# Other hidden pairs of a gated feed-forward projection take the seven-product form, and the sums of stored weights are issued at other moments

## The chip, the cores and the metric

The kernel runs on one core of a Trainium2 chip. Its engines work side by side: TensorE (PE, with its weight loads listed as PEld), VectorE (DVE), ScalarE (ACT), GpSimd (POOL) and SyncE (SP), which issues most of the transfers. The metric is the device time of one execution in microseconds (us); less is better. The runs before the change took 695.11 us in the median of three (695.10, 695.11 and 695.49).

## The reference

One layer of a streaming encoder on 512 positions of width 1024, all in float32. The part that the change touches is the channel mixer at the end:

```python
def causal_dwconv(x, w):            # 3 taps along the sequence
    K = w.shape[0]; S = x.shape[1]
    xp = jnp.pad(x, ((0, 0), (K - 1, 0), (0, 0)))
    y = xp[:, K - 1:K - 1 + S, :] * w[K - 1]
    for k in range(K - 1):
        y = y + xp[:, k:k + S, :] * w[k]
    return y
...
        x = x + (g_conv * y_conv + g_attn * y_attn) @ w_o[l]
        h = rms_norm(x, norm_ffn_g[l])
        up = causal_dwconv(h @ w_up[l], conv_ffn_w[l])      # 2 * 2816 columns
        a, b = jnp.split(up, 2, axis=-1)
        x = x + (jax.nn.silu(a) * b) @ w_down[l]
    return rms_norm(x, norm_f_g)
```

In front of it stand a gated short convolution and an attention branch, which the change leaves as they are.

## The kernel before, in words

**Precision.** Every float32 operand is split into a rounded high part and a rest, and a product is taken as three matmuls: high by high, rest of the weight by high, high weight by the rest of the activation. For each chunk of weights, `split()` has ACT write the high part (`wh`, line 274) and DVE the rest (`wl`, line 278) from the loaded `raw` tile. `wh` and `wl` have two buffers each, so a chunk can be split while PE works on the one before it, once PE has done with the one before that. `raw` has four buffers for P and up chunks together, and `rf` four for F chunks. Loads stand in SP's queue up to seven chunks ahead (`LOOK`), each waiting for its buffer.

**The up stage.** The 2816 hidden columns make 22 pairs `j` of two blocks, one block of `a` and one of `b`, in two phases: pairs 0 to 11, then 12 to 21. After each phase come the down products of that phase (`STEPS`, 12 and 8 steps). A normal pair is two chunks `up2j` and `up2j+1`; each block is 48 matmuls of 128 columns by 256. DVE takes the block out of its bank (`mul`, tile `fz`), multiplying by the norm; `taps` makes the convolution: one ACT instruction (line 565) and two on DVE (lines 566 and 569) into `fu`. `glu` then has ACT take the Silu of `a` (line 1212), and POOL multiplies by `b`: into `ge` for an even pair, into `go` for an odd one (lines 1217 and 1224). At an odd pair, DVE makes four sums of 128x256 out of `ge` and `go` (lines 1234 to 1239), and ACT and DVE split the results into `gh` and `gl` (lines 1243 and 1244): these are the operands of the seven-product down steps.

**Seven-product pairs.** For the pairs in `SUP`, `seven` computes both blocks for both halves of the sequence with seven products in place of eight. The pair is four chunks: P, F, P, F. A P chunk has 18 matmuls and an F chunk 24; in each, PE first does all that use `wh` (12 and 16) and then those that use `wl`. An F chunk is a set of four sums of weights, made by transfers inside DRAM and loaded like a weight. `merge` then puts the two blocks together from four banks on DVE (tiles `uz`, `ua`, `uu`, `ub`, lines 1173 to 1195). In names of rows, P12, F12, P13, F13 are the chunks of the first such pair, P14 to F15 those of the second, P16 to F17 those of the third.

**Order of the work around it.** Much of DVE's work is not issued at once but put on the list `later` with a time in us and a tag: `("e",)` for evacuations of a pair (out of the banks, taps, `glu`), `("q", q)` for the sums and splits of the gated values, `("x", q)` for those of the up stage's own operands. `run_later` takes from that list behind each split, up to a budget; `flush` and `flush_only` empty it for a tag or a bank.

**Sums of stored weights.** `make_forms` makes the F sums of a group of two steps by six transfers: `put` (SP) and `add` (POOL, adding into DRAM) in turn. `slot()` is called at each of the eight blocks of the output projection and twice at each pair, and issues what has come due: transfer `k` of group `g` is due at slot `step * k + shift * g`. `GROUPS` holds `(size, step, shift)`; key 0 is the down weights of phase 0: six groups, tiles `f18` to `f28`.

The kernel's functions that the change touches:

Of the kernel before, what the change touches and what calls it, by code (L numbers as in the profile page):

```python
# [58 lines left out]
PLAIN = [(m, k) for m in (6, 7) for k in range(*PHASES[1])]  # L59
PCUTS = (0, 8, 12, 20)  # L60

SUP = (1, 2, 5)
XF = 26
UPD = tuple(((j, q), (j, q + 1)) for j in SUP for q in (0, 2))
DOUBLES = GATES + UPD + STEPS[0] + STEPS[1]
N0 = len(GATES) + len(UPD)
GROUPS = {"gate": (2, 4, 1), "up": (2, 4, 1), 0: (2, 4, 1), 1: (2, 3, 1)}


@with_exitstack  # L70
def block_kernel(ctx, tc, xT, vecs, wv, win, wmix, wo, wup, wst, wdp, outT):
# [55 lines left out]
    n = 0  # L127
# [28 lines left out]
    later = []  # L156
# [31 lines left out]
    made, todo_bg = {}, []  # L188

    def make_forms(n0, n1, key):  # L190

        size, step, shift = GROUPS[key]
        make_forms.slot = 0
        cuts = [n0]
        for n in range(n0 + 1, n1 + 1):
            if n == n1 or n - cuts[-1] == size or len(DOUBLES[n]) != len(DOUBLES[cuts[-1]]):
                cuts.append(n)
        for g, (a, b) in enumerate(zip(cuts, cuts[1:])):
            m = len(DOUBLES[a]) * P
            f = dr.tile([P, b - a, 4 * m], F32, tag=f"f{a}", name=f"f{a}")  # L200
            w = wst[a:b].rearrange("n p c -> p n c")
            x0, x1, x2 = w[:, :, 3 * m : 5 * m], w[:, :, 5 * m : 7 * m], w[:, :, 7 * m : 8 * m]
            for n in range(a, b):
                made[n] = f[:, n - a, :]

            def put(dst, src):
                return lambda: keep(nc.sync.dma_start(dst, src))

            def add(dst, src):
                return lambda: keep(nc.gpsimd.dma_start(dst, src, accum_op=ALU.add))  # L210

            f0, f1, f2 = f[:, :, : 2 * m], f[:, :, 2 * m : 3 * m], f[:, :, 3 * m :]
            ops = (put(f0, x0), add(f0, x1), put(f1, f[:, :, :m]), add(f1, x1[:, :, m:]), put(f2, f1), add(f2, x2))
            todo_bg.extend((make_forms.slot + step * k + shift * g, op) for k, op in enumerate(ops))
        todo_bg.sort(key=lambda w: w[0])

    def slot():
# [18 lines left out]
    def flush(banks=None):  # L236

        def wanted(w):
            return set(w[2]) & set(banks) if banks is not None else True

        while any(map(wanted, later)):
            n = next(n for n, w in enumerate(later) if banks is None or wanted(w) or w[0] < len(parts))
            with after_split():
                later.pop(n)[3]()

    def flush_only(tags):

        while n := [n for n, w in enumerate(later) if set(w[2]) & set(tags)]:
            with after_split():
                later.pop(n[0])[3]()  # L250
# [137 lines left out]
    at = ExitStack()  # L388
# [62 lines left out]
    for kb in range(KB):  # L451
        x = xs[kb]
# [234 lines left out]
    n = 4 * H  # L687
    bf, me, mo = vec[:n, BF : BF + 1], vec[:n, ME : ME + 1], vec[:n, MO : MO + 1]
    z, e, o = (ap.tile([n, S], F32, tag="pp", name=nm, bufs=NPP) for nm in ("fz", "fe", "fo"))
# [56 lines left out]
    acc, bank_s, bank_t = ring(2, 0, 1), ring(3, 4), ring(5, 6)  # L746
# [25 lines left out]
    k = len(parts) + 2  # L772
    for q in (0, 2):
        f, g = x_sums(slice(q, q + 2))
# [8 lines left out]
    for idx in late:  # L783
        kind, i = divmod(idx, 4)
# [32 lines left out]
    def split_next():  # L817
        if len(parts) == chunk.n and stream[chunk.n][0] not in ("dp1", "dp2"):
            split()
# [288 lines left out]
    def turns(*ids):  # L1108
        st = list(ids)

        def f(name):
            f.last = st.pop(0)
            flush((f.last,))
            return bank(f.last, name)

        return f

    acc = turns(0, 1, *(2, 3, 4, 5) * 2, 6, 7, 0, 1, 2, 3, 4, 5)
    USETS = {1: (2, 3, 4, 5), 2: (6, 7, 0, 1), 5: (6, 7, 0, 1)}
    ssq3 = xp.tile([P, S], F32, tag="ssq", name="ssq3")  # L1120

    def place(ph, q):
# [2 lines left out]
    def up(j, ph, rb2, pu=None):  # L1125
        uu = []

        def tap(i, z):
            u = fp.tile([P, S], F32, tag="fu", name=f"fu{j}{i}", bufs=3)
            taps(u, z, CF + 3 * (2 * j + i))  # L1130
            uu.append(u)

        if j in SUP:
            c = len(GATES) + 2 * SUP.index(j)
            slot()
            seven(
                UPD[c - len(GATES) :][:2], c, {j: USETS[j]}, up_form, of="x",
                done=lambda i, banks, ids: merge(ph, j, banks, ids, rb2, tap, uu),
            )
            slot()  # L1140
            return
        evacs = []
        for i in range(2):
            slot()
            p = pu[i] if pu else block(f"up{2 * j + i}", x1h, x1l, True)
            if i and j + 1 == PHASES[ph][1]:
                split_next()
            z = [None]

            def mul(i=i, p=p, z=z):  # L1150
                z[0] = fp.tile([P, S], F32, tag="fz", name=f"fz{j}{i}", bufs=4)
                nc.vector.tensor_mul(z[0], p, rb2)

            evac = [(0.7, mul), (1.4, lambda i=i, z=z: tap(i, z[0]))]
            if i:
                evac.append((0, lambda: glu(ph, j, uu)))
            if any(("e",) in w[2] for w in later):
                later.extend((0, us, (("e",), acc.last) if x == 0 else (("e",),), f) for x, (us, f) in enumerate(evac))
            else:
                for _, f in evac:  # L1160
                    f()
# [46 lines left out]
    def glu(ph, j, uu):  # L1208
        a, b = uu
        q, k = j // 2, len(parts) - 1  # L1210
        g0 = place(ph, q)
        nc.scalar.activation(a, a, AF.Silu)
        if j == NP - 1:
            nc.scalar.activation(tbl, a[: 4 * H, :1], AF.Sqrt, scale=0.0, bias=eps[: 4 * H])
        if j % 2 == 0:
            ge = glu.even = fp.tile([P, 2, 2 * P], F32, tag="ge", name=f"ge{q}", bufs=2)
            keep(nc.gpsimd.tensor_mul(ge, a.rearrange(halves_of, h=2), b.rearrange(halves_of, h=2)))  # L1217
            return
        flush_only([("q", x) for x in range(q)])
        ge = glu.even  # L1220
        go = fp.tile([P, 6, 2 * P], F32, tag="gr", name=f"go{q}")

        def mul(eng):
            return eng.tensor_mul(go[:, 0:2, :], a.rearrange(halves_of, h=2), b.rearrange(halves_of, h=2))

        if j + 1 < PHASES[ph][1]:
            keep(mul(nc.gpsimd))
        else:
            later.append((k + 3, 0.7, (("q", q),), lambda: mul(nc.vector)))
        b11, b12 = ge[:, 0, :], ge[:, 1, :]  # L1230
        b21, b22, t1, t2, t3, t4 = (go[:, i, :] for i in range(6))

        def t13():
            nc.vector.tensor_sub(t1, b11, b12)
            nc.vector.tensor_sub(t3, b22, b12)

        def t24():
            nc.vector.scalar_tensor_tensor(t2, t1, -1.0, b22, op0=ALU.mult, op1=ALU.subtract)
            nc.vector.scalar_tensor_tensor(t4, t2, -1.0, b21, op0=ALU.mult, op1=ALU.subtract)

        def hl(src, gs):
            def f():
                nc.scalar.activation(gh[:, gs, :], src, AF.Copy)
                nc.vector.tensor_sub(gl[:, gs, :], src, gh.bitcast(F32)[:, gs, :])

            return f


        d = (2, 3, 4) if j + 1 < PHASES[ph][1] else (4, 5, 6)
        w = [(d[0], 0.85, t13), (d[0], 0.85, t24), (d[1], 0.7, hl(ge[:, : 1 + ph, :], slice(g0, g0 + 1 + NF * ph, NF)))]  # L1250
        w += [(d[x > 0 and 2 or 1], 0.7, hl(go[:, x : x + 2, :], slice(g0 + 1 + x, g0 + 3 + x))) for x in (0, 4, 2)]
        for n, us, f in w:
            later.append((k + n, us, (("q", q),), f))

    def combine(ph, i, banks, ids):

# [47 lines left out]
    for ph, (j0, j1) in enumerate(PHASES):  # L1304
        if ph:
            flush()
            acc = turns(*X * 5)
        if ph:
            make_forms(N0 + len(STEPS[0]), len(DOUBLES), ph)
        for j in range(j0, j1):  # L1310
            pu = None
            if j == 0:
                nrm = {}

                def mid():
                    nrm["c"] = rstd_col([ssq2], NT, 6, "n2")

                def late():
                    nrm["b"] = rstd_sb(rstd_bc(nrm["c"], NT, 7, "n2"), "n2")

                pu = lead(["up0", "up1"], x1h, x1l, mid, late)
            up(j, ph, nrm["b"], pu)
        assert not todo_bg
        flush((("e",),))
        seven(
            STEPS[ph], N0 + ph * len(STEPS[0]), ({0: X, 1: Y, 3: X, 2: Y}, {0: X, 1: Y, 2: Y})[ph],
            lambda q, g: (gh[:, place(ph, q) + g, :], gl[:, place(ph, q) + g, :]),
            goes_on=HELD if ph == 1 else None, stays=HELD if ph == 0 else None,
            done=lambda i, banks, ids: combine(ph, i, banks, ids),
        )  # L1330
# [188 lines left out]
```

## Time and profile before

| | before |
|---|---|
| median of three runs | 695.11 us |
| the profiled execution | 696.87 us, its span 695.0 us |
| PE busy in the span | 685.8 us (99%) |
| DVE busy | 534.6 us (77%) |
| ACT busy | 360.7 us (52%) |
| POOL busy | 181.8 us (26%) |
| granted TensorE clock | 0.996 in the mean |

The busy time of PE counts matmuls that overlap, so it says when PE had work, not how well it used it. The rows of the waits and of the timeline give the places where it had none. In rows of the profile `x48` is a count, the first two numbers of a timeline row are start and length in us, and `[1.24 <-ACT wh_P L274]` says that the engine had been idle for 1.24 us and who ended that.

### The profile page before, as it was taken

What the parts mean: (1) busy time and instruction counts of PE and PEld (TensorE: products, weight loads), DVE (VectorE), ACT (ScalarE), POOL (GpSimd) and SP (SyncE); (2) the same over time, 40 slices, a digit from 0 to 9 for tenths busy, and PEclk for the clock granted to TensorE, in tenths of its full rate; (3) what the DMA queues carried; (4) which work ended last, traced back from release to release, by engine and by line L of the source; (5) the groups of instructions that cost most, each with busy time, mean ns of one, the idle gap of its engine ahead of it and who ended that gap; (6) DMA issues with size and microseconds to landing.
All of it is one profiled execution on the core that took longest, in us unless ns stands there. A gap on an engine that the chain in (4) does not pass through costs nothing.

```text
span 695.0 us, 14638 instructions
## 1 busy us (share of the span) xinstructions
PE 685.8 (99%) x5960; PEld 684.1 (98%) x5960; DVE 534.6 (77%) x833; ACT 360.7 (52%) x568; POOL 181.8 (26%) x195
## 2 busy tenths in 40 slices
PE   9999999999999999999999999999999999999996
PEld 9999999999999999999999999999999999999996
DVE  6677887877578778869778799888774677777794
ACT  5574765554554444546555455545443344445572
POOL 6124947542020201213513134210000313221000
PEclk9999999999999999999999999999999999999998
DMA  8528999553568586785899876455647686766513
GB/s 310 219 63 292 216 242 211 130 121 92 190 137 227 164 272 201 236 302 118 128 302 279 211 178 133 116 177 179 200 127 231 141 194 157 188 173 174 156 31 122
DMA packets 60019, 127.57 MB, mean 184 GB/s; under 512 B 5376, under 2 KB 27920, under 8 KB 59696
## 3 DMA queue, kind: packets, MB, share of 16 engines
q1 hardware_dynamic: 41880, 101.51, 44.6%
q0 software_dynamic: 16832, 23.93, 21.7%
q10 hardware_dynamic: 1240, 1.19, 0.5%
q8 instruction: 47, 0.77, 0.4%
q14 instruction: 20, 0.16, 0.1%
HBM read 124.45 MB, written 41.42 MB: 239 GB/s over the span
## 4 chain that ended last, share of the span: by engine, by line
PE 93%; DVE 3%; DMA 2%; ACT 0%; issue 0%; DVEq 0%; ACTq 0%
PE dn L326 23%; PE p_up L308 21%; PE p_in L308 14%; PE p_up L326 6%; PE p_wo L308 6%; PE yc L308 3%; PE ya L308 3%; DMA raw_P<-in_wst_dram 2%; PE pa L476 2%; PE pb L478 2%; PE p_q L308 2%; PE p_k L308 2%; PE o L657 2%; PE tp L640 1%; PE pdB L308 1%; PE pdA L308 1%
## 5 line engine op out<-in xcount | busy, mean ns | idle before, releaser
L308 PE MATMUL p_up<-x1h,wl_up 128*128 128x256 f32 x464 | 90.4, 276 | 0.0
L308 PE MATMUL p_up<-x1h,wh_up 128*128 128x256 f32 x464 | 90.3, 276 | 0.0
L308 PE MATMUL p_up<-x1l,wh_up 128*128 128x256 f32 x464 | 90.3, 276 | 0.0
L210 POOL DMA_DIRECT2D f<-in_wst_dram x60 | 70.9, 1349 | 1.5 <-DMA f<-f 1.2
L308 PEld LDWEIGHTS p_up<-x1h,wl_up 128*128 128x128 f32 x464 | 69.9, 188 | 0.0
L308 PEld LDWEIGHTS p_up<-x1l,wh_up 128*128 128x128 f32 x464 | 69.8, 188 | 0.0
L308 PEld LDWEIGHTS p_up<-x1h,wh_up 128*128 128x128 f32 x464 | 69.8, 188 | 0.0
L278 DVE TENSOR_TENSOR wl_F<-raw_F,wh_F 128x1024 fp32r<-128x1024 f32 (+1 forms) x38 | 51.1, 1343 | 18.9 <-ACT wh_F L274 18.9
L274 ACT ACTIVATE wh_up<-raw_up 128x1024 fp32r<-128x1024 f32 x38 | 40.2, 1057 | 47.5 <-PE p_up L308 41.8
L274 ACT ACTIVATE wh_F<-raw_F 128x1024 fp32r<-128x1024 f32 (+1 forms) x38 | 40.0, 1053 | 36.1 <-PE dn L326 26.5
L308 PE MATMUL p_in<-xgh,wh_in 128*128 128x256 f32 x288 | 56.8, 279 | 0.0
L1217 POOL TENSOR_TENSOR ge<-fu,fu 128x512 f32<-128x512 f32 x11 | 19.8, 1798 | 140.8 <-DVE fu L569 108.7
L308 PE MATMUL p_in<-xgh,wl_in 128*128 128x256 f32 x288 | 56.6, 278 | 0.0
L308 PE MATMUL p_in<-xgl,wh_in 128*128 128x256 f32 x288 | 56.5, 278 | 0.0
L278 DVE TENSOR_TENSOR wl_up<-raw_up,wh_up 128x1024 fp32r<-128x1024 f32 x38 | 46.3, 1220 | 10.9 <-ACT wh_up L274 10.8
L274 ACT ACTIVATE wh_P<-raw_P 128x768 fp32r<-128x768 f32 (+1 forms) x38 | 31.7, 834 | 36.7 <-PE dn L326 22.8
L278 DVE TENSOR_TENSOR wl_P<-raw_P,wh_P 128x768 fp32r<-128x768 f32 (+1 forms) x38 | 36.9, 970 | 17.2 <-ACT wh_P L274 11.5
L308 PEld LDWEIGHTS p_in<-xgh,wh_in 128*128 128x128 f32 x288 | 44.7, 188 | 0.7
L326 PE MATMUL dn<-gl,wh_F 128*128 128x256 f32 x192 | 45.1, 276 | 0.0
L326 PE MATMUL dn<-gh,wh_F 128*128 128x256 f32 x192 | 45.1, 276 | 0.0
L308 PEld LDWEIGHTS p_in<-xgl,wh_in 128*128 128x128 f32 x288 | 43.7, 188 | 0.0
L308 PEld LDWEIGHTS p_in<-xgh,wl_in 128*128 128x128 f32 x288 | 43.6, 188 | 0.0
(343 smaller groups left out, 2150.5 us busy)
## 6 DMA issues: line engine op xcount, KB each, us to landing
raw_up<-in_wup_dram SPq DMA_DIRECT2D x38, 512.0 KB, 5.0
raw_F<-f SPq DMA_DIRECT2D x37, 512.0 KB, 4.5
raw_P<-in_wst_dram SPq DMA_DIRECT2D x37, 384.0 KB, 4.8
raw_in<-in_win_dram SPq DMA_DIRECT2D x24, 512.0 KB, 3.6
f<-in_wst_dram POOLq DMA_DIRECT2D x37, 256.0 KB, 6.3
f<-in_wst_dram SPq DMA_DIRECT2D x18, 512.0 KB, 6.6
f<-in_wst_dram POOLq DMA_DIRECT2D x18, 512.0 KB, 8.0
f<-f SPq DMA_DIRECT2D x36, 256.0 KB, 6.1
```

The lines of the kernel that those rows point to most:

```text
L210: return lambda: keep(nc.gpsimd.dma_start(dst, src, accum_op=ALU.add))
L274: ins = nc.scalar.activation(hi, raw, AF.Copy)
L278: ins = nc.vector.tensor_sub(lo, raw, hi.bitcast(F32))
L308: keep(nc.tensor.matmul(out[:, cs], w, x[:, cs], start=start and i == 0 and c == 0, stop=stop and i == 2 and c == len(cut) - 1,))
L326: keep(nc.tensor.matmul(out, wl if x == 1 else wh, xl if x == 2 else xh, start=opens and bk not in seen, stop=closes and bk not in left,))
L476: keep(nc.tensor.matmul(pa[t][:, :VW], xt, w[:, VB:], start=start, stop=stop))
L478: keep(nc.tensor.matmul(pb[t], xt, w[:, :VB], start=start and t % 2 == 0, stop=stop and t % 2 == 1))
L640: keep(nc.tensor.transpose(tp[:, ks], pt[:, ks], ident))
L657: keep(nc.tensor.matmul(o[:, 2 * P * e + c0 : 2 * P * (e + 1)], w, x[:, kb, c0:], start=e == 0 and kb == 0 and i == 0, stop=e == 1 and kb ...
L1217: keep(nc.gpsimd.tensor_mul(ge, a.rearrange(halves_of, h=2), b.rearrange(halves_of, h=2)))
```

## The change

Three things change together.

- **Which pairs.** `SUP` names pairs 1, 4 and 8 in place of 1, 2 and 5, with other banks for them (`USETS`) and another order of banks for the normal blocks (`acc`). The number of matmuls, of splits and of loads is the same.
- **Where sums go in the list.** `glu` inserts the sums and splits of the gated values in front of the first entry tagged `("e",)` in `later`, where it used to append them. At the last pair of a phase, if evacuations are pending, they are flushed and one more chunk is split ahead; and in front of the down steps only `("e",)` entries are flushed, where `flush` also ran other entries of `later` that had come due.
- **When the down weights' sums are made.** The six transfers of a group come due at slots 0, 3, 14, 18, 22 and 26 (plus the group's number) in place of 0, 4, 8, 12, 16 and 20.

```diff
-SUP = (1, 2, 5)
+SUP = (1, 4, 8)
...
-GROUPS = {"gate": (2, 4, 1), "up": (2, 4, 1), 0: (2, 4, 1), 1: (2, 3, 1)}
+GROUPS = {"gate": (2, 4, 1), "up": (2, 4, 1), 0: (2, (0, 3, 14, 18, 22, 26), 1), 1: (2, 3, 1)}
...
-            todo_bg.extend((make_forms.slot + step * k + shift * g, op) for k, op in enumerate(ops))
+            todo_bg.extend((make_forms.slot + (step * k if isinstance(step, int) else step[k]) + shift * g, op) for k, op in enumerate(ops))
...
-    acc = turns(0, 1, *(2, 3, 4, 5) * 2, 6, 7, 0, 1, 2, 3, 4, 5)
-    USETS = {1: (2, 3, 4, 5), 2: (6, 7, 0, 1), 5: (6, 7, 0, 1)}
+    acc = turns(0, 1, 6, 7, 0, 1, 6, 7, 0, 1, 2, 3, 0, 1, 2, 3, 4, 5)
+    USETS = {1: (2, 3, 4, 5), 4: (2, 3, 4, 5), 8: (4, 5, 6, 7)}
...
             if i and j + 1 == PHASES[ph][1]:
                 split_next()
+                if any(("e",) in w[2] for w in later):
+                    flush_only((("e",),))
+                    split()
...
-        for n, us, f in w:
-            later.append((k + n, us, (("q", q),), f))
+        at = next((x for x, i in enumerate(later) if ("e",) in i[2]), len(later))
+        later[at:at] = [(k + n, us, (("q", q),), f) for n, us, f in w]
...
-        flush((("e",),))
+        flush_only((("e",),))
```

Two places show how instructions move. The first is SP's queue behind the loads of the first seven-product pair (`raw_P12` to `raw_F13`); `f18` to `f28` on both sides of the arrow are the sums of the down weights. Before:

```order
L182 DMA raw_F13_4526<-f12_2618 128x1024
L182 DMA raw_P14_4538<-in_wst_dram 128x768
L182 DMA raw_F14_4540<-f14_2619 128x1024
L207 DMA f18_3993<-f18_3993 256x256
L207 DMA f20_3994<-f20_3994 256x256
L207 DMA f22_3995<-f22_3995 256x256
L182 DMA raw_P15_4682<-in_wst_dram 128x768
L182 DMA raw_F15_4684<-f14_2619 128x1024
L182 DMA raw_up6_4712<-in_wup_dram 128x1024
L182 DMA raw_up7_4764<-in_wup_dram 128x1024
L207 DMA f24_3996<-f24_3996 256x256
L207 DMA f26_3997<-f26_3997 256x256
```

The same place of SP's queue after the change:

```order
L182 DMA raw_F13_4527<-f12_2618 128x1024
L182 DMA raw_up4_4539<-in_wup_dram 128x1024
L182 DMA raw_up5_4677<-in_wup_dram 128x1024
L182 DMA raw_up6_4705<-in_wup_dram 128x1024
L182 DMA raw_up7_4757<-in_wup_dram 128x1024
L182 DMA raw_P14_4851<-in_wst_dram 128x768
L182 DMA raw_F14_4853<-f14_2619 128x1024
L207 DMA f18_3993<-f18_3993 256x256
L182 DMA raw_P15_4923<-in_wst_dram 128x768
L182 DMA raw_F15_4925<-f14_2619 128x1024
L207 DMA f20_3994<-f20_3994 256x256
L182 DMA raw_up10_5000<-in_wup_dram 128x1024
```

Four plain loads now stand between the two seven-product pairs, and the copies inside DRAM come behind them, one at a time.

The second place is DVE at a seven-product pair that does not stand right behind another one: the third pair in the order before (pair 5, chunks P16 to F17) and the second now (pair 4, chunks P14 to F15). `fz31` is the block `b` of pair 3, `fu31` its taps. Before:

```order
L1152 TENSOR_TENSOR fz30_5140<-p_up6_4938,rb_n2_4660 128x512
L278 TENSOR_TENSOR wl_P16_5195<-raw_P16_4988,wh_P16_5194 128x768
L1244 TENSOR_TENSOR gl_3989<-go0_4930,gh_3988 128x512 x2
L278 TENSOR_TENSOR wl_F16_5227<-raw_F16_4990,wh_F16_5226 128x1024
L278 TENSOR_TENSOR wl_P17_5255<-raw_P17_5055,wh_P17_5254 128x768
L566 SCALAR_TENSOR_TENSOR fu30_5258<-fz30_5140,vec_64,fu30_5258 128x511
L569 SCALAR_TENSOR_TENSOR fu30_5258<-fz30_5140,vec_64,fu30_5258 128x510
L278 TENSOR_TENSOR wl_F17_5283<-raw_F17_5057,wh_F17_5282 128x1024
```

DVE at the seven-product pair 4 after the change:

```order
L569 SCALAR_TENSOR_TENSOR fu30_4995<-fz30_4993,vec_64,fu30_4995 128x510
L1155 TENSOR_TENSOR fz31_5059<-p_up7_5010,rb_n2_4659 128x512
L278 TENSOR_TENSOR wl_F14_5108<-raw_F14_4853,wh_F14_5107 128x1024
L566 SCALAR_TENSOR_TENSOR fu31_5061<-fz31_5059,vec_64,fu31_5061 128x511
L1237 TENSOR_TENSOR go1_5074<-ge1_4942 128x256
L569 SCALAR_TENSOR_TENSOR fu31_5061<-fz31_5059,vec_64,fu31_5061 128x510
L278 TENSOR_TENSOR wl_P15_5138<-raw_P15_4923,wh_P15_5137 128x768
L1238 TENSOR_TENSOR go1_5074<-go1_5074,ge1_4942 128x256
L1241 SCALAR_TENSOR_TENSOR go1_5074<-go1_5074 128x256
L1247 TENSOR_TENSOR gl_3989<-ge1_4942,gh_3988 128x256
L1242 SCALAR_TENSOR_TENSOR go1_5074<-go1_5074 128x256
L278 TENSOR_TENSOR wl_F15_5166<-raw_F15_4925,wh_F15_5165 128x1024
```

Between the splits of the second P chunk and the second F chunk there now stand four instructions on `ge1` and `go1`, of which the first reads what POOL wrote; between the first F chunk and the second P chunk stand both taps of `fu31` and a sum. (Lines from 1150 on have numbers higher by three after the change.)

ACT's order at the same place, after the change, with the Silu (line 1215) of `fu30`, the first block of pair 3:

```order
L274 ACTIVATE wh_P14_5079<-raw_P14_4851 128x768
L565 ACTIVATE fu30_4995<-fz30_4993,vec_64 128x512
L1215 ACTIVATE fu30_4995<-fu30_4995 128x512
L274 ACTIVATE wh_F14_5107<-raw_F14_4853 128x1024
L565 ACTIVATE fu31_5061<-fz31_5059,vec_64 128x512
L274 ACTIVATE wh_P15_5137<-raw_P15_4923 128x768
```

The high part of F14 stands behind that Silu, which reads the last tap of `fu30` from DVE; before, the high parts of F16 and P17 had no Silu in front of them at that pair.

## The prediction

> **What bounds the kernel now.** First I read the waits of TensorE, since PE has work in 99% of the span. A row gives the total in us, the number of waits and the longest.
>
> ```profile
> PE dn L326 <- ACT wh_P L274: 1.2, 1, 1.2
> PE warm L115 <- DVE ones L107: 1.1, 1, 1.1
> PE p_up L326 <- DVE wl_up L278: 0.6, 1, 0.6
> ```
>
> The second is the start of the kernel. The other two lie in the first phase of the up stage, which the change rearranges. So I cut that phase where PE issues the first matmul of each pair: from pair 1 to the down steps, one row a pair, the last row pairs 8 to 11. Columns: the stretch, its length, busy time with instruction count of PE, PEld, DVE, ACT and POOL, the granted clock, the DMA engines' busy share, GB/s.
>
> ```profile
> 350.51:360.20 9.69, 9.69 (x88) 9.69 (x86) 8.17 (x10) 7.44 (x10) 1.30 (x1) 1.00 1.09 288
> 360.20:371.30 11.10, 9.86 (x86) 9.67 (x85) 7.61 (x11) 4.52 (x7) 1.06 (x1) 1.00 1.02 317
> 371.30:382.18 10.88, 10.88 (x98) 10.88 (x97) 10.69 (x18) 5.12 (x8) 5.47 (x5) 1.00 0.92 255
> 382.18:393.06 10.88, 10.88 (x98) 10.88 (x97) 8.61 (x13) 3.98 (x7) 3.25 (x2) 1.00 1.10 274
> 393.06:402.58 9.52, 9.52 (x86) 9.52 (x85) 7.43 (x9) 6.44 (x8) 0.00 (x0) 1.00 0.47 149
> 402.58:413.46 10.88, 10.88 (x98) 10.88 (x97) 10.88 (x17) 5.40 (x10) 5.67 (x5) 1.00 0.71 154
> 413.46:425.26 11.80, 11.18 (x99) 10.98 (x97) 11.80 (x20) 6.25 (x9) 3.12 (x2) 1.00 0.48 113
> 425.26:468.78 43.52, 43.52 (x387) 43.52 (x385) 39.08 (x60) 22.82 (x35) 11.89 (x7) 1.00 0.55 153
> ```
>
> An undisturbed normal pair takes 10.88 us (pairs 3, 4, 6, and 43.52 / 4), an undisturbed seven-product pair 9.52 (pair 5). Pairs 1, 2 and 7 lose 9.69 - 9.52 = 0.17, 11.10 - 9.52 = 1.58 and 11.80 - 10.88 = 0.92: together 2.67 us, all that this phase can give. The clock is granted in full throughout.
>
> The chain of waits shows pair 2's loss: the load of the weights P15 took 16.86 us to land, in a stretch where the DMA engines were busy all the time.
>
> ```profile
> 348.50 16.86 DMA raw_P<-in_wst_dram
> 365.46 0.85 ACT wh_P L274
> 366.36 5.11 PE dn L326 x42
> ```
>
> Pair 7's loss is DVE. In the same chain DVE comes to `wl_up` only after the gated values' splits, although ACT had the high part of these weights at 415.06.
>
> ```profile
> 418.73 0.68 DVE gl L1244
> 419.41 1.15 DVE wl_up L278
> 420.60 0.74 PE p_up L326 x4
> ...
> 414.01 1.05 ACT L274 ACTIVATE wh_up<-raw_up 128x1024 fp32r<-128x1024 f32 x1
> ```
>
> **The change part by part.** *Work:* matmuls, splits and loads keep their number; three seven-product and eight normal pairs are 3 x 9.52 + 8 x 10.88 = 115.60 us in any order. What counts is what is late.
>
> *The load stall goes: -1.58.* Behind F13, SP now issues four plain loads, then P14 and P15, whose work begins two normal pairs (21.76 us) later; even 16.86 us fits into that. The copies inside DRAM come behind them, singly. `raw_up4` stands where `raw_P14` stood, and that load made nobody wait. On POOL one more `add` stands ahead of the up stage and the second `add`s come later; nothing of PE's waits for POOL there. New load stalls are bounded by 0 and the one seen, 1.58; I take 0, since DMA shares after 402 are 0.48 to 0.71.
>
> *The DVE stall at pair 7 goes: -0.92.* Pairs 5 to 7 are now normal, three in a row behind pair 4.
>
> *What is late next: pair 4, +1.8.* DVE's prices, as distances between starts of consecutive rows:
>
> ```profile
> 410.87 1.21 DVE L278 TENSOR_TENSOR wl_up<-raw_up,wh_up 128x1024 fp32r<-128x1024 f32 x1
> 412.00 0.68 DVE L1195 SCALAR_TENSOR_TENSOR ua<-ua,rb_n 128x512 f32<-128x512 f32 x1
> 412.60 0.68 DVE L1195 SCALAR_TENSOR_TENSOR ub<-ub,rb_n 128x512 f32<-128x512 f32 x1
> 413.20 0.41 DVE L1234 TENSOR_TENSOR go<-ge 128x256 f32<-128x256 f32 x1
> 413.54 0.74 DVE L566 SCALAR_TENSOR_TENSOR fu<-ua,vec,fu 128x511 f32<-128x511 f32 x1
> 414.20 0.74 DVE L566 SCALAR_TENSOR_TENSOR fu<-ub,vec,fu 128x511 f32<-128x511 f32 x1
> ...
> 394.41 1.23 DVE L278 TENSOR_TENSOR wl_F<-raw_F,wh_F 128x1024 fp32r<-128x1024 f32 x1 [3.55 <-ACT wh_F L274]
> 395.55 0.95 DVE L278 TENSOR_TENSOR wl_P<-raw_P,wh_P 128x768 fp32r<-128x768 f32 x1
> 396.42 0.75 DVE L566 SCALAR_TENSOR_TENSOR fu<-fz,vec,fu 128x511 f32<-128x511 f32 x1
> ```
>
> That is 1.13 for `wl_up`, 0.60 for 512 columns, 0.34 for 256, 0.66 for a tap, 1.14 for `wl_F`, 0.87 for `wl_P`. In the new order DVE has, from `wl_up5` (free to start when pair 1 ends, some 0.4 after 360.20) to `wl_F15`: 3 `wl_up`, 2 `wl_P`, 2 `wl_F`, 12 taps, 11 of 512 columns and 13 of 256: 3.39 + 1.74 + 2.28 + 7.92 + 6.60 + 4.42 = 26.35 us, up to 386.95. PE, undisturbed, starts F15 at 360.20 + 21.76 + 9.52 - 2.72 = 388.76, and needs its `wl` after the first 16 of 24 matmuls (2.72 us for an F chunk as 24/84 of 9.52), at 390.57. That leaves 3.6 us for waits on the way, and these are the waits:
>
> ```profile
> 403.80 1.29 POOL L1224 TENSOR_TENSOR go<-fu,fu 128x512 f32<-128x512 f32 x1 [16.95 <-ACT fu L565]
> ...
> 404.14 1.49 DVE L566 SCALAR_TENSOR_TENSOR fu<-fz,vec,fu 128x511 f32<-128x511 f32 x1
> ...
> 419.55 2.15 POOL L1224 TENSOR_TENSOR go<-fu,fu 128x512 f32<-128x512 f32 x1 [8.02 <-DVE gl L1244]
> ...
> 442.11 3.57 POOL L1217 TENSOR_TENSOR ge<-fu,fu 128x512 f32<-128x512 f32 x1 [5.02 <-DVE fu L569]
> ...
> 445.03 1.19 DVE L1244 TENSOR_TENSOR gl<-go,gh 128x512 fp32r<-128x512 f32 x1
> ...
> 448.90 0.63 ACT L1212 ACTIVATE fu<-fu 128x512 f32<-128x512 f32 x1 [3.03 <-DVE fu L569]
> 449.44 1.04 ACT L274 ACTIVATE wh_up<-raw_up 128x1024 fp32r<-128x1024 f32 x1
> ...
> 450.52 1.23 DVE L278 TENSOR_TENSOR wl_up<-raw_up,wh_up 128x1024 fp32r<-128x1024 f32 x1 [1.11 <-ACT wh_up L274]
> ```
>
> The last three rows: a high part stands on ACT behind a Silu, the Silu waits for a tap on DVE, and DVE then idles 1.11 us for the high part. The new order has this twice: `wh_up7` behind the Silu of `fu20`, and `wh_F14` behind that of `fu30` (queued behind it too: `fu31`'s tap and `wh_P15`): 2 x 1.1 = 2.2. The other rows: a POOL multiply takes 1.3 alone; DVE instructions with both inputs in SBUF stretch beside it (1.49 for 0.74 and 1.19 for 0.68), or it stretches beside them (2.15, 3.57). `go0` falls on `wl_up6` (0.7), `ge1` on a `gl` (0.5). `go1` can start only after the last tap of `fu31`, when `wl_P15` follows at once: 2.15 less the 0.87 of `wl_P15` is 1.3 of idle DVE, with three small instructions and `wl_F15` queued behind, and PE waiting for that. Half a dozen hand-overs between DVE and ACT at 0.1 are 0.7. Sum 2.2 + 0.7 + 0.5 + 1.3 + 0.7 = 5.4, against 3.6: F15 is 1.8 us late, part of it already at F14.
>
> The bounds of pair 4: 0, if POOL's three multiplies slip in while DVE reads PSUM (less 0.7, 0.5 and 0.6); and 3.5, if `go1` is kept out as long as the 3.57 row (1.4 more) and the others cost 0.3 more. I take 1.8, by the nearest rows.
>
> The Trainium skill, SBUF — State Buffer, section "Who interferes with whom", says that a DVE instruction with two SBUF inputs and a GpSimd instruction that reads SBUF exclude each other: whoever issues first keeps the shared port for the whole instruction. The 404.14 row agrees (it ends just 0.54 after the multiply); the 3.57 row does not go by issue order alone, since POOL was kept out over several DVE instructions. By the rule taken strictly `go1` waits for `wl_P15` only, and the sum is the same 1.8.
>
> *Pair 8, +0.3.* It has the same order behind pair 7, but DVE comes to it with nothing left over. From P16's start T: `fz71` from T + 0.2; `wl_F16` when its high part is there, T + 1.3 to T + 2.4; two taps and a sum, 1.66; `wl_P17` and the multiply 2.15 (from the last tap), to T + 6.3; four small ones 1.36; `wl_F17` 1.2: T + 8.9. PE needs it at T + 6.80 + 1.81 = T + 8.6. Bounds 0 and 1.7 (the 3.57 row again).
>
> *The rest costs nothing:* from the first down step on, DVE's and ACT's rows stand in the order of before; in phase 1, where all pairs are normal, PE had no wait.
>
> *Sum:* 2.67 lost before; 0.17 (kept) + 1.8 + 0.3 = 2.27 after. Gain 0.4 us on the profiled 696.87 (span 695.0), which lies 1.76 above the median. 695.11 - 0.4 = 694.7.
>
> **The rivals.** *Faster:* POOL's multiplies do not collide in pairs 4 and 8. For it speaks that a row such as 403.80 (1.29) lets POOL through at once, against it that DVE has hardly a gap there. Loss 0.17 to 0.9, time 692.6 to 693.3.
>
> *Slower:* `go1` and `go3` are kept out through DVE's run of instructions, as in the 3.57 row, so that DVE, waiting for them, holds back `wl_F15` and `wl_F17`. Against it: DVE itself stops at the first instruction that needs the product, which lets POOL in. Full price 1.4 + 0.3 at pair 4 and 1.4 at pair 8: 3.1 over the forecast, 697.8; it decides against the change from 1.8 over it.
>
> *Loads still late:* the copies for the down sums now meet the loads of pairs 5 to 8. Price as seen, 1.58: 696.3.
>
> *The load stall is the profiled run's own:* the profiled execution is 1.76 longer than the median, and P15 missed by little of its 16.86. Then the change gains nothing there, and the time is 694.7 + 1.6 = 696.3.
>
> **How the numbers follow.** Within 0.2% (1.4 us, about what a measurement of this kernel can tell from no change) lie the forecast, 0.42, and the two cases at 696.3, 0.05 each: 0.52. Faster 0.25. Slower 0.23. The forecast's own range is 693.8 to 696.4; to 692.9 below and 697.0 above it leaves out about 0.05 of the faster case and 0.13 of the slower one.
>
> **What would show it.** Right: no wait of PE for `wh_P` behind a load near 365; pair 7 at 10.88; pair 4 at about 11.3 and pair 8 at 9.8; DVE idle for POOL's `go` ahead of `wl_F15`, and for `wh_F14`. Wrong: pair 4 at 9.52 (the multiplies slipped in), pair 4 over 13, a load in the chain of waits, or any wait of PE outside this phase.

## The result, and the profile after

The changed kernel takes 696.89 us (median of 13 runs, 696.27 to 697.9), the kernel before 695.1 (13 runs beside them): ratio 1.0025, 95% interval 1.0018 to 1.0032. So it is slower by 1.8 us, where a gain of 0.4 was forecast. The time lies inside the range (692.9 to 697.0), but by its median just beyond the 0.2% that the prediction called no change, and on the other side of it.

The profiled execution takes 696.96 us, about the median, with a span of 695.2 us. Against the profiled execution of before (span 695.0) that is almost nothing, and this is the trap of the case: that execution was 1.76 us above the median of its kernel, and this one is not. The cut of the up stage where PE issues each pair's first matmul (columns as in the prediction; the rows are pairs 1 to 8 in order, then pairs 9 to 11 and the down steps):

```profile
350.49:360.18 9.69, 9.69 (x88) 9.69 (x87) 7.96 (x10) 7.66 (x10) 1.29 (x1) 1.00 0.74 226
360.18:371.06 10.88, 10.88 (x99) 10.88 (x98) 10.65 (x16) 4.32 (x7) 1.30 (x1) 1.00 0.68 217
371.06:381.94 10.88, 10.88 (x99) 10.88 (x98) 9.74 (x17) 5.64 (x9) 2.96 (x1) 1.00 0.38 124
381.94:393.74 11.80, 10.11 (x87) 9.72 (x86) 9.51 (x15) 7.95 (x11) 3.95 (x3) 1.00 0.47 136
...
415.50:426.38 10.88, 10.88 (x99) 10.88 (x98) 8.96 (x13) 5.75 (x9) 4.89 (x3) 1.00 0.70 179
426.38:436.29 9.91, 9.82 (x87) 9.63 (x86) 8.12 (x13) 7.43 (x10) 3.93 (x3) 1.00 0.74 180
436.29:468.94 32.65, 32.65 (x290) 32.65 (x289) 28.82 (x43) 14.30 (x22) 9.16 (x7) 1.00 0.79 204
468.94:526.06 57.12, 57.12 (x506) 57.12 (x505) 42.55 (x57) 27.07 (x33) 0.00 (x0) 1.00 0.60 184
```

Pair 7 is at 10.88, undisturbed. Pair 4 takes 11.80 and pair 8 takes 9.91, where a seven-product pair needs 9.52: 2.28 and 0.39 us are lost, with pair 1's 0.17 together 2.84. The waits of PE (total, times, longest) name the two causes in pair 4, `wh_F` and `wl_F`; the wait for `wh_v` lies at 8.79 us, at the start of the kernel, far ahead of the change:

```profile
PE dn L326 <- ACT wh_F L274: 1.0, 1, 1.0
PE warm L115 <- DVE ones L107: 1.1, 1, 1.1
PE pa L476 <- DVE wh_v L272: 0.9, 1, 0.9
PE dn L326 <- DVE wl_F L278: 0.7, 1, 0.7
```

Around pair 4 the timeline shows both as they were described: ACT's Silu of `fu30` (L1215) waits for a tap, `wh_F14` is right behind it, and DVE then idles 1.10 for `wh_F14`; later DVE idles 1.19 for POOL's product (L1227), and `wl_F15` comes only behind four small instructions that follow.

```profile
385.15 0.38 PE L326 MATMUL dn<-x1h,wh_F 128*128 128x256 f32 x1 [1.01 <-ACT wh_F L274]
...
392.69 0.39 PE L326 MATMUL dn<-x1h,wl_F 128*128 128x256 f32 x1 [0.68 <-DVE wl_F L278]
...
383.52 0.63 ACT L1215 ACTIVATE fu<-fu 128x512 f32<-128x512 f32 x1 [3.19 <-DVE fu L569]
384.06 1.04 ACT L274 ACTIVATE wh_F<-raw_F 128x1024 fp32r<-128x1024 f32 x1
...
385.13 1.23 DVE L278 TENSOR_TENSOR wl_F<-raw_F,wh_F 128x1024 fp32r<-128x1024 f32 x1 [1.10 <-ACT wh_F L274]
...
387.93 0.95 DVE L278 TENSOR_TENSOR wl_P<-raw_P,wh_P 128x768 fp32r<-128x768 f32 x1
388.15 1.88 POOL L1227 TENSOR_TENSOR go<-fu,fu 128x512 f32<-128x512 f32 x1 [8.07 <-DVE fu L569]
...
390.07 0.43 DVE L1238 TENSOR_TENSOR go<-go,ge 128x256 f32<-128x256 f32 x1 [1.19 <-POOL go L1227]
...
391.42 1.22 DVE L278 TENSOR_TENSOR wl_F<-raw_F,wh_F 128x1024 fp32r<-128x1024 f32 x1
```

The two waits add up to 1.69 by the records, the pair's length says 2.28. In this trace the records put the end of a matmul 0.28 after its issue, while issues follow at 0.113 (9.52 for 84 matmuls), and the first issues after a wait come at wider distances (0.22 behind the one at 385.15); so each of these waits costs some 0.3 more than its row says. Distances between issues are the safer measure of a loss.

### The profile page after: what moved, and what is told of

Its sections match the earlier page's. It is cut to its first block, busy times and chain, and to the rows that moved or that the text cites. A ratio compares the mean times of both kernels' runs of the same rounds, so it can differ in the third digit from the quotient of the medians.

```text
span 695.2 us, 14637 instructions
## 1 busy us (share of the span) xinstructions
PE 685.2 (99%) x5960; PEld 683.0 (98%) x5960; DVE 534.6 (77%) x833; ACT 360.2 (52%) x568; POOL 182.8 (26%) x195
## 3 DMA queue, kind: packets, MB, share of 16 engines
q10 hardware_dynamic: 1240, 1.19, 0.5%
## 4 chain that ended last, share of the span: by engine, by line
PE 91%; DVE 5%; DMA 1%; ACT 1%; issue 1%; POOL 1%; SPq 0%; DVEq 0%; ACTq 0%; POOLq 0%
PE dn L326 23%; PE p_up L308 20%; PE p_in L308 14%; PE p_up L326 6%; PE p_wo L308 6%; PE yc L308 3%; PE ya L308 3%; PE p_q L308 2%; PE p_k L308 2%; PE o L657 2%; PE pa L476 2%; PE pb L478 1%; PE tp L640 1%; PE pdB L308 1%; PE pdA L308 1%; PE s L611 1%
## 5 line engine op out<-in xcount | busy, mean ns | idle before, releaser
L278 DVE TENSOR_TENSOR wl_up<-raw_up,wh_up 128x1024 fp32r<-128x1024 f32 x38 | 48.1, 1267 | 12.0 <-ACT wh_up L274 12.0
L278 DVE TENSOR_TENSOR wl_P<-raw_P,wh_P 128x768 fp32r<-128x768 f32 (+1 forms) x38 | 36.3, 956 | 13.6 <-ACT wh_P L274 7.9
```

The lines of the kernel that those rows point to most:

```text
L278: ins = nc.vector.tensor_sub(lo, raw, hi.bitcast(F32))
```

## The experiments

The code of the change has parts that move nothing: with the sums put behind the entries of `later` instead of in front, with `flush` in place of `flush_only` ahead of the down steps, or without the extra flush at the last pair, the built program stays the same. So two things are left to tell apart: the choice of pairs, and the moments of the down weights' sums. My theory was that of the prediction: the choice of pairs removes the load stall and the stall of pair 7, and pays at pairs 4 and 8 by the splits, while the moments cost nothing. The main rival was that the load stall belonged to one execution.

### The kernel before, profiled twice more

No edit; two more profiled runs.

> The kernel before, unchanged, profiled once more. If the load stall of pair 2 belongs to the order of the loads (my step -1.58), the fourth chunk P15 is late again: pair 2 takes about 11.1 us, the span is about 695.0 and the time about 696.9. If it belonged to that one execution, pair 2 takes 9.5 to 9.7, pair 7 keeps its 11.8 (the 0.92 stall on DVE), the span is about 693.4 and the time about 695.1.

> The kernel before, profiled a third time, for the spread of the load of P15. Theory (the landing varies from execution to execution by a few us and only the longest cost PE time): landing between 13 and 17 us after its issue; PE waits only if it is over about 15.5; span 692.9 to 693.5 without the wait, up to 695 with it.

Measured: 694.71 and 695.18 us, spans 692.9 and 693.4. In the first of them, pairs 1, 2 and 7 and the whole phase:

```profile
349.90:359.59 9.69, 9.69 (x88) 9.69 (x87) 8.17 (x10) 7.44 (x10) 1.34 (x2) 1.00 1.09 290
359.59:369.11 9.52, 9.52 (x87) 9.52 (x86) 8.69 (x13) 4.92 (x7) 1.01 (x1) 1.00 1.05 322
...
411.26:423.14 11.88, 11.25 (x99) 11.06 (x97) 11.88 (x20) 6.33 (x9) 3.14 (x2) 1.00 0.50 114
349.90:466.66 116.76, 116.13 (x1024) 115.94 (x1022) 104.01 (x152) 62.07 (x88) 30.78 (x23) 1.00 0.73 199
```

Pair 2 loses nothing; pair 7 keeps its stall (1.00 here, 0.92 in the third profile). The load of P15 is late here too, but not too late. SP issues it, and ACT waits for it:

```profile
347.97 0.44 SPq L182 DMA_DIRECT2D raw_P<-in_wst_dram  x1
...
362.74 0.85 ACT L274 ACTIVATE wh_P<-raw_P 128x768 fp32r<-128x768 f32 x1 [2.53 <-DMA raw_P<-in_wst_dram]
```

ACT begins with it 14.77 us after its issue, against 16.96 in the execution that the prediction read (348.50 to 365.46); in the third profile it is 14.80 (348.75 to 363.55). ACT idles 2.5 us for it, but PE reaches P15 only 4.76 us into pair 2, and the split takes 0.85; so PE sees nothing of it as long as ACT begins within some 15.3 to 15.6 us of the issue (worked out for each of the three executions). The margin is 0.5 to 0.7 us, and the landing varies by 2. Of the 55 timed runs of before, 5 lie above 696.1; the medians of its three series are 694.9 to 695.2. So the stall is at most a rare event of this order, not a part of its usual time.

### The two halves of the change, each alone

The changed kernel with the old moments, which leaves only the choice of pairs:

```diff
-GROUPS = {..., 0: (2, (0, 3, 14, 18, 22, 26), 1), ...}
+GROUPS = {..., 0: (2, 4, 1), ...}
```

> The changed kernel with the down weights' sums at the moments of before: only the choice of pairs differs from before. Theory (the loss is the splits at pair 4 and has nothing to do with the DMA moments): pair 4 at 11.8, pair 8 at 9.9, time 696.9, ratio to before 1.0025. Rival (the moved sums delay something or crowd the loads of pairs 5 to 8): 695.1 to 696.0, ratio 1.000 to 1.001.

Measured: 699.03 us (5 runs), ratio to before 1.0057 (1.0043 to 1.007). Both theories are wrong: without the new moments the new choice of pairs is 2 us slower still. The waits of PE and the cut (pairs 2, 3 and 4) show where:

```profile
PE dn L326 <- ACT wh_F L274: 1.4, 1, 1.4
...
PE p_up L326 <- DVE wl_up L278: 0.8, 1, 0.8
...
360.19:371.07 10.88, 10.88 (x98) 10.88 (x97) 8.77 (x15) 4.35 (x7) 2.16 (x3) 1.00 1.08 331
371.07:383.07 12.00, 11.18 (x98) 10.98 (x97) 10.85 (x16) 6.32 (x10) 5.71 (x4) 1.00 0.62 169
383.07:395.67 12.60, 10.37 (x86) 9.77 (x85) 10.31 (x17) 7.91 (x11) 3.94 (x3) 1.00 0.60 144
```

Pair 3 loses 1.12, pair 4 0.80 more than in the changed kernel. The cause stands on SP ahead of pair 1. Three copies inside DRAM (L207) come between the loads of up4 and up5 (the second `raw_up` row holds up5 and up6), and ACT then waits for up5:

```profile
344.53 0.38 SPq L182 DMA_DIRECT2D raw_up<-in_wup_dram  x1
345.00 2.93 SPq L207 DMA_DIRECT2D f<-f  x3
348.03 1.35 SPq L182 DMA_DIRECT2D raw_up<-in_wup_dram  x2
...
361.62 1.06 ACT L274 ACTIVATE wh_up<-raw_up 128x1024 fp32r<-128x1024 f32 x1 [2.35 <-DMA raw_up<-in_wup_dram]
```

In the changed kernel SP issues these two loads together, and ACT takes up5 2.15 us earlier, with an idle of 0.21 that ends with PE and not with a load:

```profile
344.20 1.48 SPq L182 DMA_DIRECT2D raw_up<-in_wup_dram  x2
...
359.47 1.06 ACT L274 ACTIVATE wh_up<-raw_up 128x1024 fp32r<-128x1024 f32 x1 [0.21 <-PE dn L326]
```

SP issues up5 3.1 us later than in the changed kernel, and it also takes longer to come: ACT begins 13.6 us after the issue, where in the changed kernel the load landed after 12.2. Those 2 us stay: DVE begins pair 1's merge at 363.86 instead of 361.88 and `wl_F15` at 393.38 instead of 391.42, with the same rows and the same idle times between, so it has no slack to make them up before pair 4.

The other half, the kernel before with the new moments (the reverse edit, and its `step` made to take a list):

> The kernel before with the down weights' sums at the new moments, pairs 1, 2 and 5 kept. Theory: ratio 1.000 within 0.001, time 695.1, since PE never waits for these sums. Rival (the load of P15 is late because of copies at the old moments, and often): ratio 0.998, 693.6, and no wait of PE for a load in the profile. Rival (they take bandwidth from the loads where they now stand): ratio over 1.001.

Measured: 695.05 us (11 runs), ratio 1.0 (0.9991 to 1.0008). On the usual run the moments do nothing here, as the theory said: pair 2 at 9.52, pair 7 at 11.88. But they decide how near P15 comes to being late. At the old moments its load stands on SP's queue behind three copies; at the new ones SP issues it ahead of them, and ACT's wait for P15 ends with PE and not with the load:

```profile
346.09 0.75 SPq L182 DMA_DIRECT2D raw_P<-in_wst_dram  x1
...
362.17 0.85 ACT L274 ACTIVATE wh_P<-raw_P 128x768 fp32r<-128x768 f32 x1 [0.94 <-PE dn L326]
```

The load lands 11.5 us after its issue, some 7 us before PE would notice. So the rival was right in one half: at the old moments the sums' transfers are what brings P15 within 0.5 to 0.7 us of a stall. That the stall comes often, its other half, is not so. Whether the new moments rid this kernel of the rare long runs isn't shown: none of the 11 lies above 695.7, but by 5 in 55 only one would be expected.

### GpSimd's product in pair 4

The changed kernel with the gate product of pairs 3 and 7 on DVE:

```diff
-            keep(mul(nc.gpsimd))
+            mul(nc.vector) if j + 1 in SUP else keep(mul(nc.gpsimd))
```

> The changed kernel with the gate product of pairs 3 and 7 (go) on VectorE in place of GpSimd; nothing else changes. Theory (VectorE stands still for GpSimd's product ahead of wl_F15): the 0.68 wait for wl_F15 goes and the wait for wh_F14 stays, pair 4 at about 10.9 instead of 11.80, pair 8 at 9.6 instead of 9.91, time 695.7, ratio to before 1.001. Rival (VectorE is simply full, the product only moves its 0.6 us onto it): pair 4 within 0.3 of 11.80, time 696.6 to 697.0.

Measured: 695.16 us (11 runs), ratio to before 1.0004 (0.9995 to 1.0013). Pair 4, pair 5 and pair 8:

```profile
381.45:392.25 10.80, 9.79 (x86) 9.59 (x85) 9.70 (x16) 7.15 (x11) 0.22 (x1) 1.00 0.72 171
392.25:403.38 11.13, 11.13 (x99) 10.99 (x98) 10.94 (x17) 4.03 (x6) 1.31 (x1) 1.00 0.44 141
425.13:434.65 9.52, 9.52 (x86) 9.52 (x85) 8.91 (x14) 7.29 (x10) 0.46 (x1) 1.00 1.08 239
```

Pair 4 gains 1.00, pair 8 0.39, and 0.25 comes back in pair 5; the wait for `wh_F14` is left at 1.01. So the forecast's mechanism for F15 is the right one. On DVE the product is one short row with no idle time around it:

```profile
388.31 0.68 DVE L1227 TENSOR_TENSOR go<-fu,fu 128x512 f32<-128x512 f32 x1
388.92 0.42 DVE L1247 TENSOR_TENSOR gl<-ge,gh 128x256 fp32r<-128x256 f32 x1
...
389.92 1.22 DVE L278 TENSOR_TENSOR wl_F<-raw_F,wh_F 128x1024 fp32r<-128x1024 f32 x1
```

`wl_F15` begins 8.47 us into the pair instead of 9.48. About two thirds of that is the product: an idle time of 1.19 goes and a row worth 0.60 comes. The last third is order: one of the four small instructions (L1242, 0.34) now stands behind `wl_F15`, which the edit brought with it. So 0.68 on a full engine is cheaper than 1.88 on an idle one where DVE has to wait for the other's end.

### The first splits of pairs 4 and 8 earlier

The changed kernel with P14 and F14 (and P16, F16) split ahead of the evacuation of the half before, and the Silu behind the high part:

```diff
+            if i and j + 1 in SUP and j:
+                split()
+                split()
             z = [None]
...
-        nc.scalar.activation(a, a, AF.Silu)
+        with tc.issue_after(order["hi"]) if j + 1 in SUP and j else ExitStack():
+            nc.scalar.activation(a, a, AF.Silu)
```

> The changed kernel with the first P and F chunk of pairs 4 and 8 split ahead of the evacuations of the pair before, and its Silu behind the high part of that F chunk; the sums of that pair's gated values then come behind wl_F15. Same work. Theory (pair 4 loses 1.3 because wh_F14 stands behind a Silu, and 1.0 because wl_F15 stands behind the wait for GpSimd's product): both go, pair 4 at 9.5 to 9.9 in place of 11.80, pair 8 at 9.5 to 9.7 in place of 9.91, time 694.2 to 694.7, ratio to before 0.999. Rival (VectorE is full around pair 4, so the delay only moves to the next splits): pair 4 short but the halves of pair 5 or 6 0.5 to 1.5 over 5.44, time 695.5 to 696.5.

Measured: 695.67 us (11 runs), ratio 1.0008 (0.9999 to 1.0017). Pair 4, pair 8, and the down steps:

```profile
381.43:391.02 9.59, 9.59 (x87) 9.59 (x85) 8.41 (x13) 7.23 (x11) 4.29 (x3) 1.00 0.47 154
423.66:433.70 10.04, 9.81 (x87) 9.62 (x85) 8.86 (x14) 7.35 (x11) 4.28 (x3) 1.00 0.82 197
...
466.34:524.60 58.26, 57.41 (x507) 57.22 (x505) 44.84 (x62) 28.21 (x35) 0.00 (x0) 1.00 0.62 189
```

Pair 4 is cured (9.59); which of the two moves did it, that of the splits or that of the Silu, isn't told apart. Pair 8 is not cured: PE now waits there for `wl_P17`, since DVE comes to it late. The down steps begin with a new stall of 1.14: the rival had a point, though the place is far from where it looked. There it is the same pattern again, a high part behind a Silu, with PE waiting:

```profile
467.76 0.63 ACT L1219 ACTIVATE fu<-fu 128x512 f32<-128x512 f32 x1 [0.90 <-DVE fu L569]
468.30 1.04 ACT L274 ACTIVATE wh_F<-raw_F 128x1024 fp32r<-128x1024 f32 x1
...
469.39 0.39 PE L326 MATMUL dn<-gh,wh_F 128*128 128x256 f32 x1 [0.85 <-ACT wh_F L274]
```

Then the same with the product of pairs 3 and 7 on DVE as well:

> As the one with early splits, and the gate product of pairs 3 and 7 on VectorE. Theory: nothing is left to gain from the product once wl_F15 stands ahead of its sums, so the time is that of the early splits within 0.3 us. Rival (GpSimd's product stretches VectorE's instructions through the shared port, whatever their order): another 0.3 to 0.8 us faster.

Measured: 694.69 us (11 runs), ratio to before 0.999 (0.9981 to 0.9999), the fastest kernel of this study and ahead of both. Pair 4, pair 8, the phase and the down steps:

```profile
381.35:390.95 9.60, 9.60 (x87) 9.60 (x85) 9.60 (x15) 7.52 (x11) 1.03 (x1) 1.00 0.78 206
423.59:433.16 9.57, 9.57 (x87) 9.57 (x86) 9.12 (x14) 7.53 (x11) 1.48 (x2) 1.00 1.07 245
349.90:465.80 115.90, 115.90 (x1024) 115.90 (x1023) 107.91 (x152) 60.82 (x87) 25.90 (x21) 1.00 0.70 189
465.80:523.21 57.41, 57.41 (x507) 57.38 (x505) 43.81 (x60) 27.70 (x34) 0.00 (x0) 1.00 0.62 188
```

The theory had expected no more than 0.3 from this, the rival up to 0.8; it brought 1.0. Where the sums no longer stood between the product and `wl_F15`, DVE still stood still for GpSimd's product behind both pairs, 1.18 us each time. Behind pair 4's splits, with the early splits alone:

```profile
390.08 0.43 DVE L1242 TENSOR_TENSOR go<-go,ge 128x256 f32<-128x256 f32 x1 [1.18 <-POOL go L1231]
```

With the product on DVE both of these idle times are gone, and pair 8 and the down steps come out shorter. The rival's mechanism is not the one seen here: beside the product at pair 4 DVE's split `wl_F15` took 1.22 as elsewhere, and it was the product that stretched, to 3.32. What cost time was the waiting for its end.

One more kernel, with seven-product pairs 1, 5 and 9, does not compute the layer, so its 701.84 us tells nothing about the choice of pairs. Whether an even pair in front of a seven-product pair keeps its splits in time stays open.

## Why the prediction was wrong

All losses of the up stage, in us over 9.52 or 10.88, from the issues of PE. The last column is the time beyond 57.12 of the down steps, the medians are those of each kernel's own series:

| kernel | pair 1 | pair 2 | pair 3 | pair 4 | pair 5 | pair 7 | pair 8 | sum | down | median |
|---|---|---|---|---|---|---|---|---|---|---|
| before, execution read | 0.17 | 1.58 | 0 | 0 | 0 | 0.92 | 0 | 2.67 | 0 | (696.87) |
| before, profiled again | 0.17 | 0 | 0 | 0 | 0 | 1.00 | 0 | 1.16 | 0 | 694.9 |
| after | 0.17 | 0 | 0 | 2.28 | 0 | 0 | 0.39 | 2.84 | 0 | 696.89 |
| after, old moments | 0.16 | 0 | 1.12 | 3.08 | 0 | 0 | 0.39 | 4.77 | 0 | 699.03 |
| after, product on DVE | 0.16 | 0 | 0 | 1.28 | 0.25 | 0 | 0 | 1.69 | 0 | 695.16 |
| after, early splits | 0.16 | 0 | 0 | 0.07 | 0 | 0 | 0.52 | 0.75 | 1.14 | 695.67 |
| early splits, product on DVE | 0.17 | 0 | 0 | 0.08 | 0 | 0 | 0.05 | 0.30 | 0.29 | 694.69 |

The differences of sum and down follow the medians: after less before is 1.68 here and 1.79 in the runs, and for the other kernels, each against before in its own series, the two agree within some 0.5. (Apart from this, PE enters the up stage at 337.12 to 338.12 in these profiles. All of that spread is there within the first 40 us and differs between executions of the same program; a single span can't tell less than that.)

*The load stall goes, -1.58:* this is the step that failed. The stall stood in the profiled execution and not in the runs against which the change is timed, so there was nothing to gain. The prediction had this as its last rival, at 0.05, and gave as evidence that the execution was 1.76 over the median. That number should have decided it: a stall of 1.58 in an execution that is 1.76 too long is most simply that surplus. What the runs show in its place is a load that usually arrives 0.5 to 0.7 us before PE would wait. I took the gain from the one execution and then took the same 1.76 off once more by going from 696.87 to the median, so the sum was made against a base that had already lost the stall.

*The stall of pair 7 goes, -0.92:* right, pair 7 is at 10.88.

*Pair 4, +1.8:* right in mechanism, both waits at the named instructions; 2.28 measured. On DVE the working holds term by term, by the distances between starts: 1.19 and 1.18 for the two Silus (1.1 each), 0.80 on `wl_up6` (0.7), 0.52 on a `gl` (0.5), 1.27 for `go1` (1.3), and some 0.5 of small hand-overs (0.7). `wl_F15`, begun at 391.42 and worth 1.13, is done at 392.55, where the forecast has 386.95 + 5.4 = 392.35. The other 0.3 come on PE's side, from the first matmul behind the wait (392.69) and the wider distances after it. *Pair 8, +0.3:* 0.39. By these two and with the right base, 695.1 - 0.92 + 2.28 + 0.39 = 696.85; measured 696.89. By the forecast's own sizes it would have been 696.3, so the rest of the miss is the 0.57 by which these two terms were too small.

*The shared port:* the Trainium skill, SBUF — State Buffer, section "Who interferes with whom", lets DVE's instructions with two SBUF inputs and GpSimd's that read SBUF shut each other out. The rows after the change agree for the pair below: the split takes 2.01 where it takes 1.22 alone, and it was issued 0.37 after POOL's product. At pair 4 the order is the other way round: `go1` starts 0.22 behind `wl_P15` and takes 1.88 for 1.30, while the split keeps its 0.95.

```profile
368.55 1.30 POOL L1227 TENSOR_TENSOR go<-fu,fu 128x512 f32<-128x512 f32 x1 [8.80 <-ACT fu L1215]
368.92 2.01 DVE L278 TENSOR_TENSOR wl_up<-raw_up,wh_up 128x1024 fp32r<-128x1024 f32 x1
```

*The moments cost nothing:* true for the kernel after, but not because they have no effect. With the new pairs they are worth 1.9 us by the traces (4.77 less 2.84), because at the old moments the three copies stand ahead of up5's load on SP. The prediction looked at what stands behind the loads with the new moments, not at what would stand between them with the old.

*The rival "slower"* (the product kept out for 3.57 us, 697.8) did not come: GpSimd's product took 1.88 in front of `wl_F15`. The change is slower than before all the same, without that rival's mechanism.

## What to carry to other kernels

Before a stall of a profile is counted as gain, hold the profiled time against the median: a surplus of the stall's size suggests that the usual run doesn't have it, and a second profile of the unchanged kernel settles it. Where weights are split on two engines in turn, ask at each step what stands ahead of the high part in its queue; here a Silu that waits for a tap cost PE over 1 us at two places (1.29 of pair 4's 2.28, and 1.14 at the down steps with the early splits), and moving the split ahead of it, with a short product on the engine that waits for it, made up for what the choice of pairs had lost and 0.1% more (0.999, interval up to 0.9999). Transfers that nobody waits for still set when the loads behind them on the same queue are issued: three copies cost 1.9 us here in one order of pairs, and left a load 0.5 to 0.7 us from a stall in the other.

## What was not expected of the hardware

The same load in the same program was taken 16.96 us after its issue in one execution and 14.77 in another, with the DMA engines busy throughout in both; what makes the difference between the two stays open. Issued ahead of the three copies, it landed in 11.5. GpSimd's product of 512 columns took between 1.29 and 3.57 us in the first phase of these kernels (1.88 at the place that decided). Moving one such product, 0.68 us on the fuller engine, shortened the pair by 1.00, with one small sum moved behind the split by the same edit.
